# Seven-product units in the last pair of down-projection chunks of an encoder layer, with second tiles placed in another turn and later casts of the blocks that are transposed by transfers

## The chip, the cores and the metric

The kernel runs on one core of one Trainium2 chip. The metric is the device time of one execution in microseconds (us). Three runs of the kernel before took 1151.23, 1153.28 and 1155.58 us; their median is 1153.28 us.

## The reference

One encoder layer in float32 over 256 positions of width 2048. With `rms_norm(x, g) = x / sqrt(mean(x^2) + 1e-6) * g`:

```
u     = rms_norm(h, g_mix_pre) @ w_in                       # 2048 x 5120
mixed = [norm(attention(q,k,v)), norm(recurrence(xr) * gelu(yg))] @ w_out
h     = h + rms_norm(mixed, g_mix_post)
fn    = rms_norm(h, g_ffn_pre)
ff    = (silu(fn @ w_ffn_gate) * (fn @ w_ffn_up)) @ w_ffn_down   # width 5632
h     = h + rms_norm(ff, g_ffn_post)
gate  = sigmoid(rms_norm(h, g_ple_pre) @ w_ple_gate)        # 2048 x 2048
h     = h + rms_norm(gate * (p @ w_ple_proj), g_ple_post)
```

The change touches the second half: the feed-forward part, above all its last `@ w_ffn_down`, and the way from there into `@ w_ple_gate`.

## The kernel before

**Products.** Each float32 operand is split into a high part (a rounded cast) and a low part (what the cast left), and each product of two blocks is three matmuls: high by high, low by high, high by low. A weight tile holds two blocks of 128 x 512 (512 KB). Its life is: a transfer from HBM into a raw buffer (`load_stream`, issued by SyncE, SP), a cast to the high part `wh` on ScalarE (ACT, line 643), a subtraction that gives the low part `wl` on VectorE (DVE, line 656), then twelve matmuls on TensorE (PE, lines 694 to 696). There are four buffers for split tiles and four for raw ones (a fifth of each in parts of the run), so ACT and DVE can be at most four tiles ahead of PE.

**Units of seven.** Two weight chunks of 512 columns and the two halves of 128 positions make a 2 x 2 problem for each pair of row blocks: eight block products. In some places a Strassen-Winograd unit does it with seven. A unit has three steps on PE: `four_products` (two weight tiles, four products, twelve matmuls), `two_products` (one tile, two products) and `one_product` (one tile for the remaining product of two units). It needs sums of the weights: DVE makes two (lines 591 and 595) and a third (line 601) in `sum_stream`, and GpSimd (POOL) adds a last one by an accumulating transfer (`last_sum`, line 612). The weights are stored with two blocks exchanged for it (`SWAPPED`). Between the fours and what follows, `made_of_four` combines the four accumulators with two copies on ACT and four subtractions on DVE; each later product of the group waits for it (`group.made`). `Group.issue` writes the order: `FOURS` says at which step of a group the fours of the *next* group are put, `TAKEN` at which step its own twos and ones. Before, the last group of the feed-forward part (down chunks 2 and 3 of the last third of the hidden width) has no such unit, and its first plain pair is put into the group ahead of it (`nxt.pair(0)`, line 511).

**Second tiles.** The second tile of a unit's fours (the one with the third sum) doesn't use a raw buffer but one of five places (`lower_tile`): 0 and 1 lie where the first half of `h` was (it is spilled to HBM), 3 and 4 where half of `mg` was, 2 in the tile `ple`. They are dealt in turn at line 2082. Once the last `two_products` has run (`last_two`, line 774), `h` is loaded back in two transfers of 1 MB, put down 3 and 15 us after it (lines 775 and 776); `ple`'s spilled half is loaded back some time after the last ones tile is split (line 664).

**The order of the work** is written by a planner on the host: `Plan` keeps a clock for each engine, each task is a generator that yields an operation with an estimated cost, and the operation that can start first (with an offset `late` that works as a priority) is issued next. Each engine then runs its instructions strictly in the order in which they were issued. An operation that is issued early, on a wrong estimate, holds up all that is behind it on its engine.

**From the feed-forward part to the gate.** `next_norm` adds the normalised result to `h`, and `h` has to be transposed into `hT_ffn_hi` and `hT_ffn_lo` for the products with `w_ple_gate`. Twelve of sixteen blocks go through PE transposes; the last four (`c = 3`, `turn_h`, line 1590) are transposed in 32 x 32 squares by DVE and moved by sixteen transfers of 32 KB (`moved`, line 333: twelve issued by POOL, four by SP), then ACT and DVE split them into `hi` and `lo` (`gained_split`, lines 317 and 319). The planner takes `plan.now` behind the transfers as the time at which that split can be issued. PE needs these blocks from the thirteenth gate tile on. The same `turn_h` serves the step into the feed-forward part (`nxt is hF`).

Of the kernel before, what the change touches and what calls it, by code (L numbers as in the profile page):

```python
# [37 lines left out]
PARTS = ((0, 4), (4, 8), (8, 11))  # L38
SEVEN_KS = (0, 2, 4)
RING = 5  # L40
DOWN_KS = (0, 2, 4, 6)
# [5 lines left out]
    *(  # L47
        (
            lambda c: (("w_ffn_down", c), ("w_ffn_down", c + 1)),
            (0, 2) if f0 != PARTS[-1][0] else (0,),  # L50
            [4 * f0 + k for k in (DOWN_KS if f0 != PARTS[-1][0] else DOWN_KS[:2])],
        )
        for f0, _ in PARTS
# [19 lines left out]
LATE = 0.8  # L73
EARLY = 3
SOON = 2.0
ADDED = 6.0
AHEAD = 5
ISSUE = 160
# [148 lines left out]
def dve(n, take=None, give=None):  # L227
    return ("dve", COST["dve"] + 0.00104 * n, None, take, give)
# [11 lines left out]
def layer(ctx: ExitStack, tc: tile.TileContext, a: dict, out: bass.AP):  # L240
# [5 lines left out]
    plan = Plan(wr=R_BUFS, w=W_BUFS, sm=SM_BUFS, acc=4, ev=1, mid=2, bt=2, m2=1, mt=1, sq=1, T0=1, T1=1, T4=1, **{f"{s}{j}": n for s, m, n in (("p", 5, 1), ("t", 4, 0)) for j in range(m)}, wr0=1, w0=1)  # L246

    def f32(t):
        return t.bitcast(F32)
# [11 lines left out]
    lower = {}  # L261
# [20 lines left out]
    def raw_kind(i):  # L282
        if i in lower:
            return f"p{lower[i]}"
        return f"wr{more_raws[i]}" if i in more_raws else "wr"
# [13 lines left out]
    def col(name, i):  # L299
        c = VEC_COLS[name][0] + i  # L300
        return vec[:, c : c + 1]
# [69 lines left out]
    def done(event):  # L371
        event.t = plan.now
# [47 lines left out]
    def seg(chunk, w, n0, lhs, ks, first=True, last=True, after=None):  # L420
        s = (chunk, lhs, ks, first, last, after, len(tiles))
        for k, _ in ks:
            tiles.append((w, k, n0))
        segs.append(s)
# [11 lines left out]
    class Group:  # L436
# [36 lines left out]
                self.last[j] = (late, i, j, js, self.lhs.ev_sums)  # L473
            segs.append((one_product, self, js, i))

        own, twos, last, ahead = None, None, None, 0

        def kind(self):
            return ("up" if self.lhs is hF else "down") + str(len(self.sevens))
# [7 lines left out]
        def issue(self, nxt):  # L487
            if self.own is None:
                self.own = []
            self.twos, self.last = {}, {}  # L490
            if nxt:
                nxt.own = []
            n, m = len(self.rest), len(self.rest) - self.apart
            steps = list(TAKEN[self.kind()]) if self.sevens else []

            def take():
                for x in steps.pop(0) if steps else "":
                    if x.isdigit():
                        self.two(int(x))
                    else:  # L500
                        self.one(range(0, 2) if x == "a" else range(2, len(self.sevens)))

            take()
            for i, k in enumerate(self.rest[:m]):
                for j, at in enumerate(FOURS[self.kind(), nxt.kind()] if nxt and nxt.sevens else ()):
                    if i == at:
                        nxt.four(j)
                if i >= self.ahead:
                    self.pair(i)
                if nxt and nxt.apart and i == 1:  # L510
                    nxt.pair(0)
                    nxt.ahead = 1
                take()
            for ch, w, n0 in self.chunks if self.apart else ():
                seg(ch, w, n0, self.lhs, self.rest[m:], first=False)
            for j, x in self.last.items():
                fours[self.own[j]] = (*x, self.twos[j])
# [3 lines left out]
    }  # L521
    FOURS = {
        ("up0", "up3"): (3, 5, 7), ("up3", "up3"): (2, 3, 4), ("up3", "down4"): (2, 3, 3, 4),
        ("down4", "down4"): (1, 2, 3, 3), ("down4", "up3"): (1, 2, 3), ("up3", "down2"): (2, 4),
    }
    fours = {}

# [8 lines left out]
    def pieces(i):  # L536

        return [slice(0, 1), slice(1, 2)] if i < EARLY else [slice(0, 2)]
# [71 lines left out]
    def added(dst, src, ev):  # L610
        yield ("pool", COST["move"], None, None, None)
        nc.gpsimd.dma_start(dst, src, accum_op=ALU.add)  # L612
        plan.now += ADDED
        done(ev)
# [31 lines left out]
    def lo_stream():  # L646
        last_one = max(f[1] for f in fours.values())
        for i in range(len(tiles)):
            at_lo[0] = i
            for j in pieces(i):  # L650
                n = j.stop - j.start
                yield ev_hi[i, j.stop]
                src = raws[i] if n == 2 else raws[i][:, j, :]
                m = slice(j.start, j.start + src.shape[1])
                yield dve(src.shape[1] * N, give=gives.get(i) or raw_kind(i) if j.stop == 2 else None)
                nc.vector.tensor_tensor(  # L656
                    out=los[i][:, m, :], in0=src, in1=f32(his[i][:, m, :]), op=ALU.subtract
                )
                done(ev_lo[i, j.stop])
            raws.pop(i)  # L660
            if i == last_one:
                done(ev_ple)
            if i == half_end:
                plan.add(reload_half(), plan.now + 46.0)
            if i in fours:
                plan.add(last_sum(i), plan.now, -2 * SOON)

# [50 lines left out]
    def four_products(group, j, i):  # L718
# [16 lines left out]
        if last:  # L735
            plan.add(made_of_four(group), plan.clk["pe"] + plan.SEM, -SOON)
            plan.run()

    def made_of_four(group):
# [5 lines left out]
        def second():  # L745
            yield act(N)
            nc.scalar.copy(q7, v)
            done(there)
# [8 lines left out]
        nc.vector.tensor_tensor(out=v, in0=u, in1=q7, op=ALU.subtract)  # L757
        plan.add(second(), plan.now, -SOON)
        yield dve(N)
# [773 lines left out]
    def next_norm(sub, nxt, rstd, ev_rstd, g_next):  # L1533
# [24 lines left out]
        for c in range(4):  # L1558
# [12 lines left out]
            if c >= TURNED:  # L1571
                plan.add(turn_h(c, hi, lo, nxt, sub.gname), plan.now, -SOON)
        yield nxt.ev[4 * TURNED - 3]
# [16 lines left out]
    def turn_h(c, hi, lo, nxt, gname):  # L1590

        for t in range(NT):
            yield dve(N, take=None if t else "mid")
            if not t:
                e = mid_tile()
            nc.vector.transpose(out=e[:, t, :], in_=t2["h"][:, t, c * N : (c + 1) * N])
        there = Event()
        mT = yield from moved(e, there, "mt", mT_tile, turn=False, pool=(0, 1, 2) if nxt is hP else ())
        plan.free["mid"].append(plan.now)
        yield there  # L1600
        for b in range(4):
            kk = 4 * c + b
            yield from gained_split(
                *(x[:, kk, :].rearrange("p (t q) -> p t q", t=NT) for x in (hi, lo)), mT[:, b],
                col(gname, kk), give="mt" if b == 3 else None,
            )
            done(nxt.ev[kk])
# [34 lines left out]
    def reload_half():  # L1642
        yield dma(1024)
        nc.sync.dma_start(t2["ple"][:, :, 0 : D // 2], half_spill)
        done(ev_half_back)
# [68 lines left out]
    hP = Act()  # L1714
# [16 lines left out]
    def mid_tile():  # L1731
        return t2["pool"].tile([P, NT, N], F32, tag="mid", name="mid", bufs=2)
# [4 lines left out]
    def up_post(f, mid, kk0, g, soon):  # L1737

        def post(ch):
# [12 lines left out]
            yield there  # L1752
            plan.add(carried(mid, kk0, mT), plan.now + (0.5 if soon else {0: 12.0, 9: 6.0}.get(f, 3.0)), -SOON if soon else 0.0)
        return post
# [120 lines left out]
    for part, (f0, f1) in enumerate(PARTS):  # L1875
        mid = Mid(f"mid{part}")
        last_part = part == len(PARTS) - 1
        for f in range(f0, f1):
            slot = ring()
            g = Chunk(gate_post(f), slot=slot)  # L1880
            u = Chunk(up_post(f, mid, (f - f0) * 4, g, f == f1 - 1), late=(-3 if f == f1 - 1 else -1) * SOON, slot=slot)
            groups.append(Group(
                [(g, "w_ffn_gate", f * N), (u, "w_ffn_up", f * N)], hF, KS,
                SEVEN_KS if f in SEVEN_F else (),
            ))
        ks = [(f0 * 4 + k, k) for k in range(0, (f1 - f0) * 4, 2)]
        for c in range(0, 4, 2):
            slot = ring()
            end = last_part and c
            groups.append(Group(  # L1890
                [
                    (Chunk(
                        sub_post(ffn, c + i, True, after_ffn) if last_part
                        else down_post(part, c + i), slot=slot,
                    ), "w_ffn_down", (c + i) * N)
                    for i in range(2)
                ],
                mid, ks, () if end else DOWN_KS[: 2 if last_part else 4], apart=2 if end else 0,
                after=load_sqrt if end else None,
            ))  # L1900
    n_ffn = len(segs)
# [160 lines left out]
    last = Chunk(None)  # L2062
# [9 lines left out]
    n = 0  # L2072
# [6 lines left out]
        if i % (W_BUFS + MORE_W) < MORE_W:  # L2079
            more_w[i] = i % (W_BUFS + MORE_W)  # L2080
    for n, i in enumerate(sorted(lower)):
        lower[i] = (2, 3, 4, 0, 1)[n % RING]
    first_slot = {i: n % 2 for n, i in enumerate(sorted(fours))}
    for i, (_, last, _, js, _, two) in fours.items():
        ev_load[i], ev_load[i + 1] = Event(), Event()
# [2 lines left out]
    twos = [(j, i) for f, g, j, i in (s for s in segs if s[0] is two_products)]  # L2088
# [31 lines left out]
    with tc.manual_schedule():  # L2120
# [16 lines left out]
        chunk, lhs, ks, _, _, _, i0 = segs[-1]  # L2137
# [76 lines left out]
```

## Time and profile before

| what | us |
|---|---|
| median of three runs | 1153.28 |
| the profiled execution's own time | 1154.53 |
| its span, first to last instruction | 1152.7 |
| PE busy | 1139.3 (99%) |
| DVE busy | 923.4 (80%) |
| ACT busy | 722.0 (63%) |
| POOL busy | 145.7 (13%) |
| DMA | 268 MB, 232 GB/s on average |

How to read it: times in the rows are counted from the span's start. A matmul's shown duration is longer than its share of PE, because the next one starts before it has ended; the distance of two starts is its cost. The products of the last down group end at 1041 us, those of the gate begin at 1048 and end at 1144. In brackets stand the idle time of the engine ahead of a row and what ended it.

### The profile page before, as it was taken

The numbers are of one execution on the slowest core, as the hardware profiler recorded it, in microseconds if no ns is written. First come the engines' busy times: TensorE is split into PE (matmuls) and PEld (weight loads), VectorE is DVE, ScalarE is ACT, GpSimd is POOL, SyncE is SP. The second block draws the span as 40 slices with busy tenths as digits, with TensorE's granted clock in tenths as the row PEclk, the third lists the DMA queues.
The fourth block names the chain that finished last, engine by engine and source line by source line (L and its number), as shares of the span: only waits on it lengthen the run. The fifth ranks groups of instructions, "written<-read, shape, count | busy, mean of one in ns | idle before, by whom it ended". The sixth has DMA issues, their size and how long they took to land.

```text
span 1152.7 us, 15162 instructions
## 1 busy us (share of the span) xinstructions
PE 1139.3 (99%) x5199; PEld 946.3 (82%) x5199; DVE 923.4 (80%) x1161; ACT 722.0 (63%) x954; POOL 145.7 (13%) x232
## 2 busy tenths in 40 slices
PE   9999999999999999999999999999999999999897
PEld 7888888888888888888888888888888888888786
DVE  6578786888468779998988898989988888769474
ACT  7777777876447645656566556666555655557473
POOL 0000000000000033142110223312111303101000
PEclk9999999999999999999999999999999999999999
DMA  9867665546685996787877786897887678866661
GB/s 323 287 188 224 186 180 191 178 150 207 226 287 176 316 291 210 239 243 218 282 259 221 248 239 213 252 273 238 259 303 247 200 246 271 287 237 213 200 216 73
DMA packets 110270, 267.97 MB, mean 232 GB/s; under 512 B 36272, under 2 KB 43184, under 8 KB 108784
## 3 DMA queue, kind: packets, MB, share of 16 engines
q1 hardware_dynamic: 96304, 243.17, 62.2%
q0 software_dynamic: 13456, 23.48, 10.3%
q8 instruction: 40, 0.66, 0.2%
q10 hardware_dynamic: 432, 0.35, 0.1%
q14 instruction: 38, 0.31, 0.1%
HBM read 249.12 MB, written 9.44 MB: 224 GB/s over the span
## 4 chain that ended last, share of the span: by engine, by line
PE 94%; ACT 2%; DVE 2%; DMA 1%; SPq 0%; issue 0%; ACTq 0%
PE acc L696 24%; PE acc L695 24%; PE acc L694 24%; PE acc L707 6%; PE acc L706 6%; PE acc L705 6%; PE tr L330 1%; ACT wh L643 1%; DVE wl L656 1%; DMA wr<-in_w_ple_gate 1%; DMA sq<-ev 0%; ACT junk L1579 0%; DMA wr<-in_w_in 0%; PE pg L362 0%; PE pg L361 0%
## 5 line engine op out<-in xcount | busy, mean ns | idle before, releaser
L656 DVE TENSOR_TENSOR wl<-wr,wh 128x1024 fp32r<-128x1024 f32 (+1 forms) x304 | 363.1, 1208 | 107.9 <-ACT wh L643 106.5
L643 ACT CAST wh<-wr 128x1024 fp32r<-128x1024 f32 (+1 forms) x304 | 314.9, 1043 | 183.8 <-PE acc L695 133.3
L349 POOL DMA_DIRECT2D mT<-mid x164 | 96.3, 600 | 625.6 <-ACT wh L643 482.3
L695 PE MATMUL acc<-wh,hT_mix_lo 128*128 128x512 f32 x420 | 163.6, 390 | 0.3 <-DVE hT_mix_lo L319 0.3
L694 PE MATMUL acc<-wh,hT_mix_hi 128*128 128x512 f32 x420 | 163.7, 390 | 0.0
L696 PE MATMUL acc<-wl,hT_mix_hi 128*128 128x512 f32 x420 | 163.4, 389 | 0.0
L696 PE MATMUL acc<-wl,hT_hi 128*128 128x512 f32 x320 | 124.5, 390 | 0.0
L694 PE MATMUL acc<-wh,hT_hi 128*128 128x512 f32 x316 | 124.4, 394 | 0.0
L695 PE MATMUL acc<-wh,hT_lo 128*128 128x512 f32 x316 | 123.1, 390 | 0.0
L643 ACT CAST wh<-ple 128x1024 fp32r<-128x1024 f32 (+1 forms) x65 | 64.9, 1005 | 75.8 <-DVE ple L595 44.6
L695 PEld LDWEIGHTS acc<-wh,hT_mix_lo 128*128 128x128 f32 x420 | 78.8, 188 | 17.2 <-DVE hT_mix_lo L319 1.0
L696 PEld LDWEIGHTS acc<-wl,hT_mix_hi 128*128 128x128 f32 x420 | 78.8, 188 | 16.4
L694 PEld LDWEIGHTS acc<-wh,hT_mix_hi 128*128 128x128 f32 x420 | 78.8, 188 | 16.3
L656 DVE TENSOR_TENSOR wl<-ple,wh 128x1024 fp32r<-128x1024 f32 (+1 forms) x65 | 75.2, 1160 | 7.6 <-ACT wh L643 7.4
L696 PEld LDWEIGHTS acc<-wl,hT_hi 128*128 128x128 f32 x320 | 60.1, 188 | 12.9
L695 PEld LDWEIGHTS acc<-wh,hT_lo 128*128 128x128 f32 x316 | 59.4, 188 | 11.5
L694 PEld LDWEIGHTS acc<-wh,hT_hi 128*128 128x128 f32 x316 | 59.4, 188 | 11.4
L696 PE MATMUL acc<-wl,hT_ffn_hi 128*128 128x512 f32 x104 | 41.4, 398 | 3.5 <-DVE wl L656 3.5
L612 POOL DMA_DIRECT2D ple<-in_w_ffn_up x27 | 24.1, 893 | 161.6 <-DVE wl L656 121.3
L694 PE MATMUL acc<-wh,hT_ffn_hi 128*128 128x512 f32 x104 | 41.5, 399 | 0.3 <-ACT hT_ffn_hi L317 0.3
L695 PE MATMUL acc<-wh,hT_ffn_lo 128*128 128x512 f32 x104 | 41.1, 395 | 0.0
L643 ACT CAST wh<-third 128x1024 fp32r<-128x1024 f32 x30 | 31.5, 1051 | 11.3 <-PE acc L695 5.7
(439 smaller groups left out, 2441.8 us busy)
## 6 DMA issues: line engine op xcount, KB each, us to landing
wr<-in_w_in SPq DMA_DIRECT2D x77, 512.0 KB, 4.5
wr<-in_w_ffn_gate SPq DMA_DIRECT2D x74, 512.0 KB, 5.2
wr<-in_w_ffn_down SPq DMA_DIRECT2D x58, 512.0 KB, 5.7
wr<-in_w_ffn_up SPq DMA_DIRECT2D x51, 512.0 KB, 5.0
wr<-in_w_out SPq DMA_DIRECT2D x32, 512.0 KB, 4.0
wr<-in_w_ple_gate SPq DMA_DIRECT2D x32, 512.0 KB, 4.5
lower<-in_w_ffn_up SPq DMA_DIRECT2D x20, 512.0 KB, 6.3
lower<-in_w_ffn_down SPq DMA_DIRECT2D x16, 512.0 KB, 5.9
```

Of the source, the lines that this page charges most:

```text
L330: nc.tensor.transpose(tr[:, b, t * P : (t + 1) * P], e[:, t, sl], ident)
L349: (nc.gpsimd if i in pool else nc.sync).dma_start(dst[32 * j : 32 * j + 32, :, :, i, :], src[32 * i : 32 * i + 32, :, :, j, :],)
L612: nc.gpsimd.dma_start(dst, src, accum_op=ALU.add)
L643: nc.scalar.copy(his[i][:, 0 : src.shape[1], :] if n == 2 else his[i][:, j, :], src)
L656: nc.vector.tensor_tensor(out=los[i][:, m, :], in0=src, in1=f32(his[i][:, m, :]), op=ALU.subtract)
L694: nc.tensor.matmul(accs[t], hi[:, sl], his[i][:, j, :], start=st, stop=False, **group)
L695: nc.tensor.matmul(accs[t], lo[:, sl], his[i][:, j, :], start=False, stop=False, **group)
L696: nc.tensor.matmul(accs[t], hi[:, sl], los[i][:, j, :], start=False, stop=sp, **group)
L705: nc.tensor.matmul(dst, x[0], wh, start=start, stop=False, skip_group_check=seeded)
L706: nc.tensor.matmul(dst, x[1], wh, start=False, stop=False, skip_group_check=seeded)
L707: nc.tensor.matmul(dst, x[0], wl, start=False, stop=stop, skip_group_check=seeded)
```

## The change

- `SWAPPED`, and `DOWN_KS[: 2 ...]` in place of `()` for the last group: it gets two units of seven, for row pairs 0 and 2, as the group ahead of it has.
- `Group.issue`: the early plain pair of the last group is gone (`ahead`); its two fours are put at steps 2 and 3 of the group ahead (`("down2", "down2"): (2, 3)`).
- `("up3", "down2")` goes from `(2, 4)` to `(4, 4)`: in the last gate/up group the two fours of the group that follows are both put at step 4.
- `reload_half` is put down 22 us after the last ones tile is split; it was 46. The last ones tile now belongs to the last group.
- `turn_h` ends with a new task, `split_turned`, that holds the splits of the moved blocks. For the step into the gate (`hP`) it is ready `LATER = 6.0` us after the planner's end of the transfers, for the step into the feed-forward part at once.
- The places of second tiles are dealt `3, 4, 0, 1, 2` in turn, the last two of all on 0 and 1.

```diff
@@ SWAPPED
-            (0, 2) if f0 != PARTS[-1][0] else (0,),
+            (0, 2),
             [4 * f0 + k for k in (DOWN_KS if f0 != PARTS[-1][0] else DOWN_KS[:2])],
@@
+LATER = 6.0
@@ class Group
-        own, twos, last, ahead = None, None, None, 0
+        own, twos, last = None, None, None
@@ Group.issue
-                if i >= self.ahead:
-                    self.pair(i)
-                if nxt and nxt.apart and i == 1:
-                    nxt.pair(0)
-                    nxt.ahead = 1
+                self.pair(i)
                 take()
@@ FOURS
-        ("down4", "down4"): (1, 2, 3, 3), ("down4", "up3"): (1, 2, 3), ("up3", "down2"): (2, 4),
+        ("down4", "down4"): (1, 2, 3, 3), ("down4", "up3"): (1, 2, 3), ("up3", "down2"): (4, 4), ("down2", "down2"): (2, 3),
@@ lo_stream
             if i == half_end:
-                plan.add(reload_half(), plan.now + 46.0)
+                plan.add(reload_half(), plan.now + 22.0)
@@ turn_h
         mT = yield from moved(e, there, "mt", mT_tile, turn=False, pool=(0, 1, 2) if nxt is hP else ())
         plan.free["mid"].append(plan.now)
         yield there
+        plan.add(split_turned(c, mT, hi, lo, nxt, gname), plan.now + (LATER if nxt is hP else 0.0), -SOON)
+
+    def split_turned(c, mT, hi, lo, nxt, gname):
         for b in range(4):
             kk = 4 * c + b
             yield from gained_split(
@@ the last down group
-                mid, ks, () if end else DOWN_KS[: 2 if last_part else 4], apart=2 if end else 0,
+                mid, ks, DOWN_KS[: 2 if last_part else 4], apart=2 if end else 0,
@@ places
-        lower[i] = (2, 3, 4, 0, 1)[n % RING]
+        lower[i] = (3, 4, 0, 1, 2)[n % RING] if n < len(lower) - 2 else n + 2 - len(lower)
```

## The prediction

> **What bounds the kernel now.** I read the page first, then TensorE's waits, then the order of time on PE, ACT and DVE around the one wait that counts.
>
> ```profile
> PE 1139.3 (99%) x5199; PEld 946.3 (82%) x5199; DVE 923.4 (80%) x1161; ACT 722.0 (63%) x954; POOL 145.7 (13%) x232
> PE acc L696 <- DVE wl L656: 3.5, 1, 3.5
> ```
>
> PE is the bound: 13.4 of 1152.7 us of the span are not PE. So only two things can shorten the kernel much: fewer matmuls, or PE's few idle places. The largest wait inside the products is a single one of 3.5 us, for a low part of a weight tile. In the order of time on PE, with two rows from 961 us ahead and the gate's first, which give the distance of matmuls:
>
> ```profile
> 961.13 0.39 PE L705 MATMUL acc<-wh,sums 128*128 128x512 f32 x1
> ...
> 963.85 0.39 PE L694 MATMUL acc<-wh,hT_mix_hi 128*128 128x512 f32 x1
> ...
> 1048.26 0.50 PE L694 MATMUL acc<-wh,hT_ffn_hi 128*128 128x512 f32 x1 [0.27 <-ACT hT_ffn_hi L317]
> ...
> 1075.25 0.39 PE L695 MATMUL acc<-wh,hT_ffn_lo 128*128 128x512 f32 x1
> 1079.10 0.77 PE L696 MATMUL acc<-wl,hT_ffn_hi 128*128 128x512 f32 x1 [3.46 <-DVE wl L656]
> ...
> 1082.86 0.40 PE L696 MATMUL acc<-wl,hT_ffn_hi 128*128 128x512 f32 x1
> ```
>
> Between the first two rows lie twelve matmuls, the fours of one unit: 2.72 us, 0.2267 each. The stall costs more than its 3.46 us. The matmul behind 1075.25 would have begun at 1075.48; it began at 1079.10, 3.62 late. Then nine starts take until 1082.86, 3.76 us, where nine full-speed ones take 2.04: another 1.72. The granted clock, 1.00 in the stretches quoted further down, is 0.94 here:
>
> ```profile
> 1080.00:1100.00 20.00, 20.00 (x84) 16.39 (x84) 10.44 (x10) 8.57 (x9) 0.00 (x0) 0.94 0.74 238
> ```
>
> Together **5.34 us**. Why the low part was late is seen on ACT and DVE:
>
> ```profile
> 1068.78 1.05 ACT L643 CAST wh<-wr 128x1024 fp32r<-128x1024 f32 x1 [1.54 <-DMA wr<-in_w_ple_gate]
> 1075.13 0.51 ACT L317 ACTIVATE hT_ffn_hi<-mT,vec 128x256 fp32r<-128x256 f32 x1 [5.30 <-DMA wr<-in_w_ple_gate]
> 1075.55 1.03 ACT L643 CAST wh<-wr 128x1024 fp32r<-128x1024 f32 x1
> ```
> ```profile
> 1075.68 0.48 DVE L319 SCALAR_TENSOR_TENSOR hT_ffn_lo<-mT,vec,hT_ffn_hi 128x256 fp32r<-128x256 f32 x1 [7.18 <-ACT hT_ffn_hi L317]
> ...
> 1077.83 1.22 DVE L656 TENSOR_TENSOR wl<-wr,wh 128x1024 fp32r<-128x1024 f32 x1
> ```
>
> The tile cast at 1068.78 gets its low part only at 1077.83, because DVE's queue has the splits of the moved blocks ahead of it and these wait for transfers. (The releaser named is a weight load; the instruction reads `mT`, so I take the move.) The moves themselves:
>
> ```profile
> 1060.26 5.17 POOL L349 DMA_DIRECT2D mT<-mid  x9 [68.81 <-ACT wh L643]
> ...
> 1067.63 1.16 POOL L349 DMA_DIRECT2D mT<-mid  x2 [0.56 <-issue]
> DMA to landing us min/median/max: 1.9/6.1/9.0
> ```
>
> (The landing is that of all sixteen.) The last is issued at about 1068.2 and lands 6 to 7 us later, when ACT moves on. The planner prices a move at 0.44 us and 2.0 at the end, so twelve from 1060.26 end at 1067.6 in its book, 7.5 us too early; just there it put the split.
>
> **The later split.** From 1067.6 the split moves to 1073.6 in the planner's order. What can be issued in between is the next casts, which need a split buffer: four tiles, one freed per 2.72 us. PE begins the late tile at 1075.02 (one matmul ahead of the row at 1075.25), the tenth gate tile by count from 1048.26. Its predecessors by three and two end at 1069.6 and 1072.3, so two more casts and their subtractions, tiles eleven and twelve, pass ahead of the split. Low parts then: tile ten at 1071.1 (needed 1075.5), eleven at 1072.3 (needed 1078.2), twelve at 1074.9 (needed 1080.9). The moved blocks, first needed by tile thirteen at 1083.2, land at 1075.1, and four split pairs of 0.5 us pipelined are done by 1077.7. Behind them waits tile thirteen's cast (1.05 and 1.22), done by 1080. The cover is 3 to 4 us on every edge, so I cost the stall at zero afterwards: **−5.34**. If the order puts only one cast ahead, tile twelve's low part comes at about 1079, still in time; if none, nothing changes, bound 0. POOL and SP issue the same sixteen moves as before; nothing is moved past them. The feed-forward side of `turn_h` has a delay of zero and the same priority: 0.
>
> [...]
>
> **Two units of seven.** Each replaces 24 matmuls by 21: six less, 6 x 0.2267 = **−1.36**. The places in the old trace:
>
> ```profile
> 988.33 0.39 PE L705 MATMUL acc<-wh,mid2h 128*128 128x512 f32 x1
> ...
> 991.05 0.39 PE L694 MATMUL acc<-wh,mid2h 128*128 128x512 f32 x1
> ...
> 1001.93 0.39 PE L705 MATMUL acc<-wh,mid2h 128*128 128x512 f32 x1
> ...
> 1041.37 0.39 PE L694 MATMUL acc<-wh,pTh 128*128 128x512 f32 x1
> ```
> ```profile
> 800.00:960.00 160.00, 160.00 (x708) 132.48 (x707) 140.99 (x157) 92.20 (x99) 32.27 (x48) 1.00 0.76 249
> 960.00:1000.00 40.00, 40.00 (x178) 33.14 (x177) 31.79 (x33) 22.98 (x27) 9.48 (x15) 1.00 0.95 319
> 1000.00:1040.00 40.00, 40.00 (x178) 33.11 (x177) 25.74 (x28) 21.36 (x31) 0.00 (x0) 1.00 0.66 226
> 995.00:1015.00 20.00, 20.00 (x90) 16.57 (x89) 12.98 (x15) 11.07 (x15) 0.00 (x0) 1.00 0.86 307
> ```
>
> The twos of the group ahead stand at 988.33 to 991.05, its ones at 1001.93. In the new order a plain pair (24 matmuls, 5.44 us) leads to the ones at 996.5, the new fours stand at 997.9 and 1006.0, the group ends at 1014.2 as now, the last group's twos run from 1019.6 to 1022.3, its ones at 1027.8, and it ends at 1040.0 (now 1041.4). What it adds to the other engines: three tiles more to split (ACT 1.05, DVE 1.22 each), six sums of weights (0.69 each on DVE) and the combining. Of the combining the first and the last rows in the group ahead are
>
> ```profile
> 977.37 0.58 ACT L753 COPY u<-acc 128x512 f32<-128x512 f32 x1
> ...
> 980.78 0.69 DVE L762 TENSOR_TENSOR acc<-acc,u 128x512 f32<-128x512 f32 x1
> ```
>
> so 4.1 us from first to last, with four DVE rows of 0.69. DVE gets 3.7 + 4.1 + 2.8 = 10.6 us more; in 1000 to 1040 it has 14.3 idle (in a window's row stand the busy times of PE, weight loads, DVE, ACT and POOL, the granted clock, the DMA's share and GB/s), and 36.3 of 40 (91%) compares with 88% in 800 to 960, where PE lost nothing. ACT's 4.3 fit easily. The one wait added is the new group's first plain pair on `group.made`: fours end at 1008.7, the pair follows at 1014.2, so 4.1 has 5.4 to be done in. Behind it on DVE stand the additions of the chunk that ends at 1011.5. If both additions (1.4) go ahead it still holds, if the gains do too (1.3 more) PE loses 1.4: bounds 0 and 1.4, I take 0. Two accumulating transfers of 256 KB come on POOL, idle there, 15 us ahead of use: 0. Bytes rise by 0.5 MB.
>
> **The first pair's fours together.** They now need four tiles in 5.4 us at about 972. There, in the old trace:
>
> ```profile
> 971.58 0.62 ACT L311 CAST mid2h<-mT 128x512 fp32r<-128x512 f32 x1 [6.70 <-DMA mT<-mid]
> ```
> ```profile
> 975.18 0.39 PE L707 MATMUL acc<-wl,sums 128*128 128x512 f32 x1
> ...
> 976.54 0.39 PE L707 MATMUL acc<-wl,mid2h 128*128 128x512 f32 x1
> ```
> ```profile
> 973.18 1.23 DVE L656 TENSOR_TENSOR wl<-ple,wh 128x1024 fp32r<-128x1024 f32 x1 [0.26 <-ACT wh L643]
> 974.65 1.23 DVE L656 TENSOR_TENSOR wl<-third,wh 128x1024 fp32r<-128x1024 f32 x1 [0.24 <-ACT wh L643]
> ```
>
> ACT stood 6.7 us for a move, and the low parts of the second unit's fours were ready at 974.4 and 975.9, for products that read them first at 975.2 and 976.5. With two fours there, four buffers are filled ahead of ACT's wait; the second tile of the first fours is then cast at about 972.1 to 973.2, its low part is done at 974.4, and PE wants it at 973.8: 0.6 late at least, up to 2 if the loads (DMA at 95% in 960 to 1000) push more. If the planner casts it ahead of the wait, 0. Bounds 0 and 2; I take **+0.3**, nearer 0, because the loads for this unit can go out 2.7 us sooner than the old ones of the second unit.
>
> **The reload of `h`.** It follows the last twos, which move from 991.05 to 1022.3.
>
> ```profile
> 993.74 0.42 SPq L1848 DMA_DIRECT2D h<-h_spill  x1
> ...
> 1006.03 0.42 SPq L1848 DMA_DIRECT2D h<-h_spill  x1
> ...
> 1041.59 0.60 SPq L1644 DMA_DIRECT2D ple<-ple_spill  x1
> DMA to landing us min/median/max: 7.7/8.0/8.3
> DMA to landing us min/median/max: 7.8/9.7/11.7
> ```
> ```profile
> 1044.57 0.88 DVE L1565 SCALAR_TENSOR_TENSOR h<-mg,ro_ffn,h 128x256 f32<-128x256 f32 x2
> ```
> ```profile
> 1046.81 1.17 PE L330 MATMUL tr<-ident,h 128*128 128x128 f32 x8
> ```
>
> The two go out 2.7 and 15.0 us behind the twos, so at 1025 and 1037.3 now; the landings quoted are those of `h` and, below, of the two parts of `mg`. DVE wants the second half with the second of two operations at 1044.57 − 1.36 + 0.4 = 1043.6. Landing after 8.0 is 1045.3: 1.7 late, and behind that operation stands all of DVE's queue, and PE, whose transposes follow the embedding's products without slack. The two old landings were in busy DMA (307 GB/s in 995 to 1015 by the windows; 226 in 1000 to 1040), so 6 to 8 is likely; bounds 0 and 1.7 (4.1 by the slowest `mg` part plus). I take **+0.8**. [...]
>
> **Places, reload of `ple`.** The places are the same ring begun one on, with the last two where `h` comes back: 0. The half of `ple` goes out at about 1043.5 instead of 1041.6, wanted only by the first gate chunk's end after 1090: 0, though it shares DMA with the loads of the first gate tiles; bound 1.
>
> **Sum.** −5.34 − 1.36 + 0.3 + 0.8 = **−5.6** on the profiled execution's 1154.53 (1152.7 of span and 1.8 around it): 1148.9. The median of the runs is 1.25 lower; if their stall is as long, 1147.7 comes out, if it is just the stall that is shorter there, 1148.9. I say **1148.0**.
>
> **Rivals.**
> 1. *All covered.* `h` is back in time and the fours together cost nothing: −6.7, from 1154.53 and 1153.28 to 1147.8 and 1146.6; say 1146.8. For it: bounds of 0 in both added terms. Against: the 8.0.
> 2. *Crowding at the fours together.* With a loss of 2 there and 1.4 at the combining, −5.6 + 1.7 + 1.4 = −2.5, which is 3.1 above the forecast: 1151. For it: margins of 0.8 and 0.6 us in the old rows of 973 and 975. Against: PE had no wait there.
> 3. *The change doesn't do what it says*: the moves land even later, or the casts that pass ahead are held by raw tiles not yet loaded, so that the stall stays. Then −1.36 + 1.1 = −0.3, 5.3 above the forecast: 1153.3. For it: ACT also waited 1.54 for a raw tile at 1068.78.
> 4. *Slower: `h` comes back too late.* The second MB shares the DMA with two more of gain and `ple`. A landing 11.7 after issue is 1049.0, 5.4 late; with a cold restart of 1.7 that is 7.1 against a gain of 6.7, so 1154.9 on the profiled scale. It decides from 5.0 us late on, a landing 11.3 after issue; at 17 it is 0.5% slower. Against: no 1 MB reload of `h` took over 8.3.
>
> **Chances and range.** My forecast 0.42, rivals 0.28, 0.10, 0.13, 0.07. A difference of 0.5% (5.8 us) is about what a measurement of this kernel can tell from none; the border is at 1147.5. Rival 1 lies below it, and about a third of the forecast's spread: 0.42 for faster. Slower by over 0.5% is the tail of rival 4 and what I haven't seen: 0.06. The rest, 0.52, is within. The range 1144.5 to 1153.5 leaves out rival 4 and the outer ends of 1 and 3; the forecast's own is 1146.5 to 1150.
>
> **What would show it.** Right: no wait of PE for `wl` near 1075 and no row of 0.6 us there, ACT with two casts between 1069 and the moved blocks; matmul rows six fewer; the last group's twos at about 1020 and its end at about 1040. PE's idle at the first transposes tells the price of `h`, rows at 972 that of the fours. Wrong: a stall of over 2 us anywhere in 960 to 1090, or the old one still there.

## The result and the profile after

The changed kernel takes **1147.07 us** (median of six runs, 1146.44 to 1149.05); six runs of the kernel before, taken beside them, have a median of 1153.59 (1151.23 to 1155.58). The ratio is 0.9945 with an interval of 0.9931 to 0.996: 6.5 us less, 0.55%. The forecast was 1148.0. The profiled execution took 1146.92 us, its span is 1145.1, 7.6 less than before's.

PE's row on the page after, and TensorE's waits of 0.2 us and more, all of them (what waited, on what; us in total, times, longest):

```profile
PE 1136.3 (99%) x5193; PEld 944.7 (82%) x5193; DVE 932.7 (81%) x1174; ACT 727.2 (63%) x959; POOL 147.7 (13%) x234
```
```profile
PE final L2056 <- ACT diag L2054: 2.0, 1, 2.0
PE warm L2123 <- POOL ones L296: 1.1, 1, 1.1
PE acc L692 <- DVE hT_mix_lo L320: 0.3, 1, 0.3
PE tr L331 <- DVE h L1562: 0.2, 1, 0.2
PE acc L704 <- DVE wl L653: 0.2, 1, 0.2
```

Matmuls are six fewer (5199 before). The wait of 3.5 us for a low part is gone; the only one left for `wl` is 0.2 us long, and it stands at the fours (line 704; lines are three or so lower than before). The place of the old stall, in the order of time on ACT, DVE and PE of the changed kernel:

```profile
1064.96 1.05 ACT L640 CAST wh<-wr 128x1024 fp32r<-128x1024 f32 x1 [0.72 <-DMA wr<-in_w_ple_gate]
1066.76 1.05 ACT L640 CAST wh<-wr 128x1024 fp32r<-128x1024 f32 x1 [0.74 <-DMA wr<-in_w_ple_gate]
1068.99 1.05 ACT L640 CAST wh<-wr 128x1024 fp32r<-128x1024 f32 x1 [1.17 <-DMA wr<-in_w_ple_gate]
1070.95 1.06 ACT L640 CAST wh<-wr 128x1024 fp32r<-128x1024 f32 x1 [0.91 <-DMA wr<-in_w_ple_gate]
1072.28 0.91 ACT L318 ACTIVATE hT_ffn_hi<-mT,vec 128x256 fp32r<-128x256 f32 x2 [0.27 <-DMA wr<-in_w_ple_gate]
```
```profile
1067.85 1.23 DVE L653 TENSOR_TENSOR wl<-wr,wh 128x1024 fp32r<-128x1024 f32 x1 [0.57 <-ACT wh L640]
...
1073.18 0.87 DVE L320 SCALAR_TENSOR_TENSOR hT_ffn_lo<-mT,vec,hT_ffn_hi 128x256 fp32r<-128x256 f32 x2
```
```profile
1073.25 0.39 PE L692 MATMUL acc<-wh,hT_ffn_lo 128*128 128x512 f32 x1
1073.48 0.39 PE L693 MATMUL acc<-wl,hT_ffn_hi 128*128 128x512 f32 x1
```

Before, ACT stood 5.30 us in front of the split of the moved blocks with the casts behind it. Now the casts go ahead as their weights land, two more of them than before (those of the eleventh and twelfth gate tile, at 1068.99 and 1070.95) pass ahead of the split, the longest pause is 1.17 us, and when the split's turn comes at 1072.28 the blocks are there. DVE makes the low part of the tenth gate tile at 1067.85, where it was 1077.83. PE's starts are 0.23 us apart throughout.

The group of products ahead of it ends 2.13 us sooner than before's 1041.37, with a new small gap at its new fours:

```profile
996.47 0.39 PE L703 MATMUL acc<-wh,sums 128*128 128x512 f32 x1
997.03 0.50 PE L704 MATMUL acc<-wl,sums 128*128 128x512 f32 x1 [0.18 <-DVE wl L653]
...
998.77 0.50 PE L704 MATMUL acc<-wl,mid2h 128*128 128x512 f32 x1
...
1039.24 0.39 PE L691 MATMUL acc<-wh,pTh 128*128 128x512 f32 x1
```

The distance from 996.47 to 997.03 is 0.56 where a step is 0.23: 0.33 lost, and another 0.22 just ahead of 998.77. The few steps right behind each of the two are a little long as well (0.34 us and less), so that in all the matmuls from 985 to 1012 us take 0.85 more than their number times 0.2267. So of the span's −7.6, −5.34 are the stall, −1.36 the six matmuls, +0.85 this place, +0.13 the gate's first matmuls and −0.26 the last 200 matmuls with what follows them. About −1.6 more comes from the stretch ahead of 240 us, which the change does not reach: that part of the profiled execution of before ran longer than in any other execution profiled here (they differ by up to 1.2 among themselves). The sum is −7.6. A difference of that kind between two executions is scatter and not the change.

### The profile page after: what moved, and what is told of

It reads as the page before. It is cut to its first block, busy times and chain, and to the rows that moved or that the text cites. A ratio compares the mean times of both kernels' runs of the same rounds, so it can differ in the third digit from the quotient of the medians.

```text
span 1145.1 us, 15184 instructions
## 1 busy us (share of the span) xinstructions
PE 1136.3 (99%) x5193; PEld 944.7 (82%) x5193; DVE 932.7 (81%) x1174; ACT 727.2 (63%) x959; POOL 147.7 (13%) x234
## 4 chain that ended last, share of the span: by engine, by line
PE 93%; DVE 3%; DMA 2%; ACT 2%; issue 1%; SPq 0%; POOL 0%; ACTq 0%; DVEq 0%; POOLq 0%
PE acc L693 23%; PE acc L692 23%; PE acc L691 23%; PE acc L704 6%; PE acc L703 6%; PE acc L702 6%; DVE wl L653 1%; PE tr L331 1%; DMA mg<-part 1%; ACT wh L640 1%; DMA sq<-ev 0%; PE warm L2123 0%; PE pg L362 0%; PE pg L363 0%; PE pg L361 0%
## 5 line engine op out<-in xcount | busy, mean ns | idle before, releaser
L653 DVE TENSOR_TENSOR wl<-wr,wh 128x1024 fp32r<-128x1024 f32 (+1 forms) x300 | 358.6, 1209 | 100.7 <-ACT wh L640 98.9
L640 ACT CAST wh<-wr 128x1024 fp32r<-128x1024 f32 (+1 forms) x300 | 310.8, 1043 | 171.8 <-PE acc L692 114.2
L640 ACT CAST wh<-ple 128x1024 fp32r<-128x1024 f32 (+1 forms) x68 | 68.2, 1008 | 77.2 <-DVE ple L592 47.3
L653 DVE TENSOR_TENSOR wl<-ple,wh 128x1024 fp32r<-128x1024 f32 (+1 forms) x68 | 79.2, 1164 | 10.1 <-ACT wh L640 9.7
```

Of the source, the lines that this page charges most:

```text
L640: nc.scalar.copy(his[i][:, 0 : src.shape[1], :] if n == 2 else his[i][:, j, :], src)
L653: nc.vector.tensor_tensor(out=los[i][:, m, :], in0=src, in1=f32(his[i][:, m, :]), op=ALU.subtract)
```

## The experiments

All of them compute the whole reference. Where one number is given, it is of one execution, with its span in brackets; 1145.1 is the span to compare it with. Line numbers are those of the changed kernel. "Lost" PE time is the distance of two starts less 0.2267; where a stretch is named, it is the whole stretch less its number of steps times 0.2267.

### 1. The later split alone, and everything but the later split

The changed kernel without the delay:

```diff
-LATER = 6.0
+LATER = 0.0
```

> The changed kernel with the delay of the moved blocks' split set from 6.0 to 0.0; nothing else. Only some fifteen lines of ACT's and DVE's order differ, PE's and the transfers' orders are the same. Theory A (the split, issued too early, holds up the weight casts behind it on ACT and DVE): two casts stand ahead of the split instead of four, DVE has one subtraction and then three low parts of moved blocks ahead of the subtraction of tile ten. With the moves landing at about 1072 to 1073 that low part is done at about 1076 to 1077, wanted at 1073.4: PE stalls 2.7 to 3.6 us there, with or without the 1.7 us of the slow restart, so 1150 to 1152.5 us. Theory B (the stall was caused by weight loads that were late in crowded DMA, and went away because the reloads of h and ple moved): no stall, 1147 us, as the changed kernel.

The kernel before with nothing but the new task `split_turned` and its delay of 6:

```diff
+LATER = 6.0
@@ turn_h
+        plan.add(split_turned(c, mT, hi, lo, nxt, gname), plan.now + (LATER if nxt is hP else 0.0), -SOON)
+
+    def split_turned(c, mT, hi, lo, nxt, gname):
         for b in range(4):
```

> The kernel before with the later split of the moved blocks alone (6.0 us), no new units, old places, old reloads. Theory A: the stall of 3.6 us and its restart of 1.7 us are gone, 5.3 less than before: 1148.3 us. Theory B: the stall stays, 1153.6 us. In both, 1.36 us are not gained, since no matmul is saved.

Without the delay: 1153.22 us (ten runs, 1150.27 to 1155.16) against 1153.38 of the kernel before (thirteen runs); ratio 1.0, interval 0.999 to 1.0009. The whole gain is gone. With the delay alone: 1147.64 (four runs, 1147.36 to 1148.13), ratio 0.9947, interval 0.9931 to 0.9964. On PE, ACT and DVE of the kernel without the delay:

```profile
1074.04 0.39 PE L692 MATMUL acc<-wh,hT_ffn_lo 128*128 128x512 f32 x1
1077.42 0.50 PE L693 MATMUL acc<-wl,hT_ffn_hi 128*128 128x512 f32 x1 [2.99 <-DVE wl L653]
...
1078.09 0.63 PE L692 MATMUL acc<-wh,hT_ffn_lo 128*128 128x512 f32 x1
...
1081.07 0.48 PE L693 MATMUL acc<-wl,hT_ffn_hi 128*128 128x512 f32 x1
```
```profile
1067.98 1.05 ACT L640 CAST wh<-wr 128x1024 fp32r<-128x1024 f32 x1 [1.59 <-DMA wr<-in_w_ple_gate]
...
1073.45 0.51 ACT L318 ACTIVATE hT_ffn_hi<-mT,vec 128x256 fp32r<-128x256 f32 x1 [4.42 <-DMA mT<-mid]
```

The stall is back in its old place, 3.15 us lost in it and 1.4 in the seven slow steps behind it, and this time the releaser is named: it is the move into `mT`, not a weight load. That settles what the prediction had taken from the operands alone. It also tells how the parts add up: the delay is worth 5.7 us by itself (1147.64 against 1153.38), and everything else next to nothing without it. What everything else brings on top of the delay the medians can't tell: the changed kernel's are 1147.07 here and 1147.92 in experiment 7, one on each side of 1147.64. The traces can, further down.

### 2. How much delay

```diff
-LATER = 6.0
+LATER = 3.0
```

> The changed kernel with the delay at 3.0. Three casts stand ahead of the split instead of four. By the prediction's margins (one cast ahead is enough, since tile twelve's low part is then done at about 1075.5 and wanted at 1078.8 on the new scale) PE loses nothing: the time of the changed kernel, no gap above 0.3 us near 1073. If the margin is thinner than I read it, a gap of 1 to 3 us there.

```diff
-LATER = 6.0
+LATER = 12.0
```

> The changed kernel with the delay at 12.0. Seven casts stand ahead of the split, the last of them needs the split buffer that PE frees at about 1078.3, so the four splits run from about 1079.4 to 1081.4 on ACT and the first low part is done at about 1081.1; PE wants the first moved block at about 1081.0. Theory A: a loss of 0 to 0.5 us at 1081, none at 1073. If the delay is what matters and not the order (a longer one is only better), no loss at all; if a late split costs what an early one did, 3 to 5 us.

The casts ahead of the split are counted from the ninth gate tile on, the one at 1064.96 in the changed kernel: two without the delay, as before the change, and four with 6. With 3: 1145.83 (span 1144.0), three casts ahead of the split, no gap at 1073. With 12: 1147.93 (span 1146.1), seven casts ahead, and the splits in one run on ACT, still ahead of the thirteenth tile's products:

```profile
1080.34 1.71 ACT L318 ACTIVATE hT_ffn_hi<-mT,vec 128x256 fp32r<-128x256 f32 x4
```

PE loses nothing there either. The 2.1 us between the two executions lie elsewhere: 1.2 ahead of 240 us, where both have the same work, and 0.93 in 985 to 1012, where the one with 3 loses nothing. So the delay has a plateau that reaches at least from 3 to 12; three casts ahead are as good as four or seven, as the cover worked out in the prediction said.

### 3. The reload of `h`

```diff
-            plan.add(reload("h", 1), plan.clk["pe"] + 15.0)
+            plan.add(reload("h", 1), plan.clk["pe"] + 19.0)
```

> The changed kernel with the second half of h put down 19 us behind the last twos instead of 15. In SP's order it then stands behind two more gate loads, so it goes out at about 1039.4 instead of 1033.8. In the changed kernel the two halves land 6.2 and 7.7 us after issue, about 1.6 to 3 us before DVE wants the second one (1043.1). My reading (the slack is real and this small; behind it there is no cover): landing at 1045.6 to 1047.1, PE idle 2.5 to 4 us at the first transposes, and perhaps a slow restart of up to 1.7: 1149.5 to 1152.5 us. The rival reading (the embedding's products and other work cover a late half): under 0.5 us lost.

1150.95 (span 1149.1), 4.0 more than the changed kernel's span. The reload and its user, first in the changed kernel (SP and DVE in order of time, then the landings of the reload), then with the delay (SP, PE and DVE):

```profile
1033.78 0.43 SPq L1848 DMA_DIRECT2D h<-h_spill  x1
...
1042.73 1.28 DVE L1562 SCALAR_TENSOR_TENSOR h<-mg,ro_ffn,h 128x256 f32<-128x256 f32 x3
```
```profile
DMA to landing us min/median/max: 6.2/6.9/7.7
```
```profile
1039.51 0.38 SPq L1848 DMA_DIRECT2D h<-h_spill  x1
...
1045.97 0.33 PE L331 MATMUL tr<-ident,h 128*128 128x128 f32 x1 [1.12 <-DVE h L1562]
1047.50 1.34 PE L331 MATMUL tr<-ident,h 128*128 128x128 f32 x7 [1.20 <-DVE h L1562]
...
1045.44 0.48 DVE L1562 SCALAR_TENSOR_TENSOR h<-mg,ro_ffn,h 128x256 f32<-128x256 f32 x1
1046.96 1.67 DVE L1562 SCALAR_TENSOR_TENSOR h<-mg,ro_ffn,h 128x256 f32<-128x256 f32 x4 [1.04 <-DMA h<-h_spill]
```

In the changed kernel the second half is in at 1033.78 + 7.7 = 1041.5 (the first landed after 6.2), and the second of DVE's three operations wants it at about 1043.1: 1.6 us in hand. In the experiment it goes out 5.7 later (two more loads stand ahead of it in SP's queue) and comes at 1046.96, 3.8 past that time; PE loses 3.8 between 999 and 1140: 2.6 in two waits at the transposes and 1.2 in slow steps behind them. Not all of it is the transfer itself. With the later estimate the planner puts two weight subtractions ahead of DVE's additions to `h`, so the first addition comes at 1045.44 and not at 1042.73, and PE's first wait is for that one; the second follows the transfer. Together that is the fourth rival's mechanism, here with its price in one execution, and the change stays 1.6 us clear of it.

### 4. The first pair's fours, and the last group's

```diff
-("up3", "down2"): (4, 4)
+("up3", "down2"): (2, 4)
```

> The changed kernel with the first pair's fours put back to steps 2 and 4 (they are both at 4). My prediction priced the fours together at a loss of 0.3 (0 to 2) at about 972; the changed kernel shows no gap there. If they cost nothing, this run has the changed kernel's time within the scatter of single runs (1146.4 to 1149) and no gap in 955 to 985. If putting them together was needed (the sums of the new first unit in the last group, or the places, come late otherwise), gaps appear in 955 to 1000, 0.5 to 3 us in all.

```diff
-("down2", "down2"): (2, 3)
+("down2", "down2"): (3, 3)
```

> The changed kernel with the last group's fours both at step 3 of the group ahead (they are at 2 and 3). The changed kernel loses 0.33 and 0.22 us at 997 and 998, at the low parts of the first of these fours; the run without delay 0.86 there, the run with delay 3 nothing. If the place is too early for DVE, which is just then behind with moved blocks (a wait of ACT for a move at 993 to 995), the gaps at 997 are gone and 0 to 0.9 us are gained; if four tiles in 5.4 us crowd DVE at 1003 to 1009, where chunk additions follow at 1009, gaps of 0.5 to 1.5 us appear there instead.

With the first pair's fours apart as before: 1148.52 (span 1146.7), nothing lost at 972, but 1.46 + 0.16 at the new fours in place of 0.55:

```profile
998.83 0.50 PE L704 MATMUL acc<-wl,sums 128*128 128x512 f32 x1 [1.31 <-DVE wl L653]
```

In the whole stretch from 985 to 1012 it is 1.89. The third sum for the new fours (line 598) is the row that moved on DVE, first in the changed kernel, then with the fours apart, where it stands behind the splits of moved blocks of the hidden state:

```profile
991.01 0.69 DVE L598 TENSOR_TENSOR wr<-wr,lower 128x512 f32<-128x512 f32 x1
```
```profile
996.35 0.69 DVE L314 TENSOR_TENSOR mid2l<-mT,mid2h 128x512 fp32r<-128x512 f32 x1 [0.78 <-ACT mid2h L312]
996.96 0.68 DVE L598 TENSOR_TENSOR wr<-wr,lower 128x512 f32<-128x512 f32 x1
```

Its two loads go out at 978.22 and 981.74 there, against 975.81 and 980.03 in the changed kernel. So `(4, 4)` costs nothing where I looked for its price (PE loses nothing at 970 to 976 in the changed kernel either) and saves something 25 us later, by one execution: 1.89 lost against 0 to 1.43 in those of the same units with the fours together. With the last group's fours together too: 1147.03 (span 1145.2), one gap of 0.27 at 997 in place of two, no other. The difference is within what two executions differ by: no result.

### 5. The turn of the places

```diff
-        lower[i] = (3, 4, 0, 1, 2)[n % RING] if n < len(lower) - 2 else n + 2 - len(lower)
+        lower[i] = (2, 3, 4, 0, 1)[n % RING] if n < len(lower) - 2 else n + 2 - len(lower)
```

> The changed kernel with the second tiles' places dealt in the old turn (2, 3, 4, 0, 1), the last two still on 0 and 1. The places before the last are then 0 and 1 as well, so the last two loads wait for the low parts of the group ahead's twos (at about 985 to 987); in the changed kernel the first of these loads goes out at 975.8 and at 992.5 the second. My prediction priced the new turn at 0. If the earlier place matters, the load at 975.8 goes out 10 us later, all loads behind it on SP with it, and PE stalls at 980 to 1000 for 1 to 4 us; if the order absorbs it, under 0.5 us.

And the same with the first pair's fours apart, so that the units stand there without either helper:

```diff
-("up3", "down2"): (4, 4)
+("up3", "down2"): (2, 4)
-        lower[i] = (3, 4, 0, 1, 2)[n % RING] if n < len(lower) - 2 else n + 2 - len(lower)
+        lower[i] = (2, 3, 4, 0, 1)[n % RING] if n < len(lower) - 2 else n + 2 - len(lower)
```

> The changed kernel with both helpers of the units undone: the first pair's fours at 2 and 4 again, the places in the old turn; the units and the later split stay. Alone, the fours apart lost 1.6 us at 997 (0.9 to 1.0 more than the changed kernel) and the old turn 2.75 and a slow restart of 1.7 (3.7 more). Both lie at the same spot, the first fours of the last group, so they need not add: 1150 to 1152 us, against 1147.6 for the kernel before with the later split alone. If so, the units are worth less than nothing without their two helpers. If the time is 1148 or below, the helpers were needed one at a time only.

With the old turn: 1150.27 (span 1148.5), 3.4 more. SP's queue of the changed kernel, then SP, DVE and PE of the one with the old turn:

```profile
975.81 0.42 SPq L548 DMA_DIRECT2D lower<-in_w_ffn_down  x1
...
983.72 8.10 SPq L350 DMA_DIRECT2D mT<-mid  x8
```
```profile
983.58 5.16 SPq L350 DMA_DIRECT2D mT<-mid  x8
988.84 0.54 SPq L548 DMA_DIRECT2D lower<-in_w_ffn_down  x1
...
990.49 0.38 SPq L548 DMA_DIRECT2D third<-in_w_ffn_down  x1
```
```profile
997.41 0.69 DVE L588 TENSOR_TENSOR ple<-third 128x512 f32<-128x512 f32 x1 [2.30 <-DMA third<-in_w_ffn_down]
998.02 1.22 DVE L653 TENSOR_TENSOR wl<-ple,wh 128x1024 fp32r<-128x1024 f32 x1
```
```profile
996.32 0.39 PE L703 MATMUL acc<-wh,sums 128*128 128x512 f32 x1
999.30 0.50 PE L704 MATMUL acc<-wl,sums 128*128 128x512 f32 x1 [2.59 <-DVE wl L653]
...
1001.62 0.63 PE L702 MATMUL acc<-wh,sums 128*128 128x512 f32 x1
...
1004.16 0.40 PE L691 MATMUL acc<-wh,mid2h 128*128 128x512 f32 x1
```

With the new turn the load of the new fours' second tile goes out 13 us sooner, ahead of the moves. In the old turn it goes out at 988.84, behind eight moves, and the loads behind it in SP's queue go out late with it; DVE then stands 2.30 us for one of them with the subtraction that PE wants behind it. PE loses 2.75, and 1.5 more in seven slow steps from 1001.03 to 1004.16. With both helpers gone: 1150.63 (span 1148.8), 2.81 lost at 997 and 1.5 in slow steps. The two losses do not add: from 985 to 1012 PE loses 4.75 with both gone, 4.70 with the old turn alone and 1.89 with the fours apart alone. Against the delay alone (1147.64) the units without their helpers cost 3.0 us, although they save six matmuls.

### 6. The reload of `ple`

```diff
-                plan.add(reload_half(), plan.now + 22.0)
+                plan.add(reload_half(), plan.now + 46.0)
```

> The changed kernel with the reload of ple's half put down 46 us after the last ones tile's split, as before the change (22 now). In SP's order it moves behind some eight gate loads, to about 1068. My prediction priced the earlier reload at 0 and said that the half is wanted only at the first gate chunk's end after 1090: no gap, the changed kernel's time (1146.4 to 1149). If the earlier reload was needed, PE or the gate's post work waits at 1085 to 1095, or the moved blocks or gate loads come late in DMA that is now fuller: 1 us or more.

1147.03 (span 1145.2), with 0.24 and 0.25 lost at 997 and nothing new: no price, as predicted.

### 7. The same delay at the other place of its kind

The gap of 0.55 at 997 has the old stall's form on a small scale. ACT of the changed kernel:

```profile
994.14 0.62 ACT L312 CAST mid2h<-mT 128x512 fp32r<-128x512 f32 x1 [5.03 <-DMA mT<-mid]
994.67 1.05 ACT L640 CAST wh<-ple 128x1024 fp32r<-128x1024 f32 x1
```

ACT stands 5.03 us for moved blocks of the hidden state, with the cast for the new fours behind. That split was put 0.5 us after the planner's end of its moves; here it is 3.5:

```diff
-            plan.add(carried(mid, kk0, mT), plan.now + (0.5 if soon else {0: 12.0, 9: 6.0}.get(f, 3.0)), -SOON if soon else 0.0)
+            plan.add(carried(mid, kk0, mT), plan.now + (3.5 if soon else {0: 12.0, 9: 6.0}.get(f, 3.0)), -SOON if soon else 0.0)
```

> The changed kernel with another split of moved blocks put later, the one of the last hidden block of each third (0.5 us after the planner's end of the moves, here 3.5). In the changed kernel ACT waits 5.0 us for those moves at 989 to 994 with weight casts behind it, and PE loses 0.55 (0 to 0.9 in the runs so far) at 997. Theory A says it is the same thing as at 1075: with two casts ahead of the split the gap at 997 goes and 0.3 to 0.9 us are gained over the changed kernel, 1146.5 us. If the split itself then comes too late for the plain pair that needs these blocks at about 999, a gap of up to 1 us appears there.

The changed kernel was run again beside it, on the same chip and in the same rounds:

> The changed kernel itself, on the same chip and in the same rounds as the run before it, to compare with: 1147.1 us; a gap at 997 of 0 to 0.9 us, none at 1073.

With the later split: 1146.15 (five runs, 1145.81 to 1147.65), ratio to before 0.9939, interval 0.9926 to 0.9951. The changed kernel beside it: 1147.92 (1147.75 to 1148.67), ratio 0.9954, interval 0.994 to 0.9968. ACT with the later split, then the changed kernel beside it:

```profile
991.03 1.05 ACT L640 CAST wh<-ple 128x1024 fp32r<-128x1024 f32 x1 [2.09 <-DVE ple L592]
...
994.93 1.15 ACT L312 CAST mid2h<-mT 128x512 fp32r<-128x512 f32 x2 [1.87 <-DMA mT<-mid]
```
```profile
995.15 0.62 ACT L312 CAST mid2h<-mT 128x512 fp32r<-128x512 f32 x1 [5.61 <-DMA mT<-mid]
```

The cast for the fours goes ahead at 991.03, and no gap is left at 997; the run beside it loses 0.69 + 0.25 there. So this version beats both kernels: by 1.8 us in the medians, of which the traces show 1.43 at the place of the edit (0 against 1.43 lost from 985 to 1012). The rest lies in other places (the two profiled executions differ by another 0.6 ahead of 240 us, where both have the same work), and I do not claim it.

## Why the prediction was right, and where its steps were not

**The stall: right in mechanism and size.** −5.34 was predicted and is what the trace shows, with the releaser as assumed. The two casts that were to pass ahead, tiles eleven and twelve, are the two that did (1068.99 and 1070.95), and the plateau shows that one would have been enough, as the prediction said. The third rival, a stall that stays, is out for this kernel; what it looks like is experiment 1 without the delay.

**The restart: rightly taken as part of the stall.** The 1.72 us behind the stall came from the trace of before, where the granted clock is 0.50 from 1079.15 to 1082.56 and 1.00 in the 3.4 us behind that, and they went with it. Shorter waits were followed by such a slow stretch too: 2.99 us without the delay by 1.4 lost in it, 2.59 with the old turn of places by 1.5. The sum left open that at the median just the stall is shorter, which gave 1148.9. No run shows that; the 1.6 us ahead of 240 are more than the whole 1.25 between the profiled execution and the median.

**The units: right in matmuls, wrong in what they bring.** Six fewer is exact, and the 1.36 us are there, but most of them are lost again. The profiled executions, from the same matmul of each (PE's 4301st, at about 946 us, ahead of the new units) to the end of the span:

| execution | from there to the end | lost from 985 to 1012 |
|---|---|---|
| the delay alone, no units | 200.0 | 0 |
| the changed kernel | 199.5 | 0.85 |
| the changed kernel again (experiment 7) | 200.0 | 1.43 |
| delay 3 (experiment 2) | 198.7 | 0 |
| the other split later too (experiment 7) | 198.5 | 0 |

Where nothing is lost, the units bring 1.3 to 1.5 us, their matmuls; where 0.85 or 1.43 is lost, 0.6 or nothing. The step that failed is "I take 0" for what the units ask of the other engines. I looked for the price at the combining, where it is 0:

```profile
1000.00:1040.00 40.00, 40.00 (x178) 33.10 (x177) 34.70 (x40) 25.76 (x36) 0.86 (x1) 1.00 0.75 248
```

(The changed kernel's windows; 178 matmuls of 0.2267 us in 40 us, no gap, and DVE busy 34.70 where I had 36.3.) It stands at the new fours, 0.85 in this execution, 0 to 1.43 in others of the same units and helpers, because a split that waits for moves holds up their cast (experiment 7). I had looked for that wait at 971 and not at 994, where the new fours stand.

**The fours together: wrong sign.** +0.3 was put on them; they cost 0 and save 0.5 to 1.9 at 997 (1.89 lost in one execution with the fours apart, 0 to 1.43 in those with them together). I weighed the unit that is pulled together and not the one that gets its loads sooner by it.

**The places: wrong.** "The same ring begun one on: 0" is true of the ring and not of the kernel with the units: undone, 3.4 us are lost. What the step left out is when each place comes free against when the new second tile has to be loaded. Nothing in the trace of before shows that tile, but the places' last readers are there, and I did not follow them.

**The reload of `h`: too dear.** +0.8 was predicted, 0.1 at most is there (the 0.2 us wait of the transposes). The size failed in the time of issue, 1033.78 and not 1037.3: I had carried the old distances from the twos (2.7 and 15.0 us) over to a place where they came out shorter (the twos end at 1021.6, the second half goes out 12.2 later). The landing was well taken for the half that counts: 7.7 us after issue, near the 8.0. The lower end of "6 to 8" was an estimate; the first half came near it, after 6.2. So the term came out near 0 by the earlier issue and not by a faster landing: issued at 1037.3, a landing after 7.7 would have been at 1045.0 and late. The reload of `ple` cost 0, as said.

**Why the sum was good all the same.** In part by luck. Two terms too dear (0.8 and 0.3, together 1.0 too much) stood against one price not seen (0.85). The helpers that I costed at nothing are worth more than the units that they help; I predicted the whole of them and so never had to separate them. The forecast of 1148.0 was 0.9 above the measured median, and rival 1 (1146.8, everything covered) 0.3 below; but that rival's "all covered" is not what happened, since 0.85 was lost at the new fours, and the second set of the changed kernel, 1147.92, is at the forecast. Nor do the runs decide on which side of 0.5% the change lies: 0.55% less in the first set, 0.46% in the second.

## What to carry to other kernels

In an engine's queue, an operation that waits for a transfer should be issued as late as its own reader allows, not as early as an estimate says that the transfer may be done: a wrong estimate of 7.5 us cost 5.3 here, while delays of 3, 6 and 12 cost nothing, and the same search at a second place paid again. A saving of a few matmuls is worth its supply only: six fewer are 1.36 us, of which 0.85 and 1.43 were lost again in two executions of the changed kernel and nothing in one where no cast was held up; without their loads and places arranged they lose 3. When a change comes as a bundle, cost each part with the others absent as well as present, or a "0" will hide the part that holds the rest up.

## What the runs showed of the hardware that was not expected

Five of the profiled executions have a slow stretch of PE behind a wait. Their mean granted clock is 0.996 or 0.997; that of the others is 0.998 or 0.999. The slow steps cost 1.72 us after the wait of 3.46 (before), 1.4 after 2.99 (without the delay), 1.5 after 2.59 (old turn of places), 1.5 after the wait in which 2.81 are lost (both helpers gone), and 1.2 with the late reload of `h`, after waits of 1.12 and 1.20. After the one wait of 1.31 with the fours apart the granted clock stayed at 1.00. Before the change the clock is 0.50 for 3.41 us, from 1079.15 on, and PE resumes at 1079.10. The fall doesn't always stand so close to the restart: with the old turn PE resumes at 999.30 and the clock falls at 1000.69. Two windows of that kernel, then two of the one with the fours apart (columns as in the prediction, the clock ahead of the DMA's share):

```profile
997.28:1000.68 3.40, 1.38 (x6) 1.05 (x6) 3.27 (x4) 1.57 (x3) 0.93 (x1) 1.00 0.36 146
1000.70:1004.10 3.40, 3.40 (x9) 2.51 (x8) 3.40 (x5) 1.74 (x2) 0.00 (x0) 0.50 0.81 166
```
```profile
997.21:1000.62 3.41, 2.10 (x10) 1.48 (x9) 3.36 (x5) 2.87 (x3) 0.93 (x1) 1.00 0.01 2
1000.63:1004.03 3.40, 3.40 (x16) 2.49 (x15) 3.40 (x5) 1.12 (x2) 0.00 (x0) 1.00 0.86 178
```

In the first window of the old turn PE was busy for 1.38 of 3.40 us, and the clock is 0.50 in the second. With the fours apart it was busy for 2.10 of 3.41, the wait of 1.31 lies whole in the first window, and the clock is 1.00 in both. What decides whether the clock falls, and when, these runs do not show. In these executions a wait of 2.59 to 3.46 us cost its length and 1.4 to 1.7 us more.
